# High and low halves of the weights side by side in one tile, features 1024 bytes apart

## The chip, the core and the metric

The kernel runs on one core of a Trainium2 chip. The time is the device time of one execution in microseconds (us). The kernel before was timed in three runs: median 1880.48 us, from 1879.29 to 1882.33 us.

## What is computed

The kernel computes one inference step of a decoder with two layers, for a prompt of 512 tokens and eight samples of eight tokens each, 576 token rows in all. The model is 1024 wide. Layer 0 mixes tokens by retention with four heads, layer 1 by multi-scale pooling. After the mixer each layer has cross-attention into 256 memory tokens and a gated feed-forward block with a causal convolution of width 3 between its two projections. Everything is float32. Cut to what the change touches, the reference is a row of products of token rows with weight matrices:

```python
proj = h @ w_in                      # retention: 1024 x 6144
out  = (silu(g) * o) @ w_out         # 2048 x 1024
k, v = hm @ wk, hm @ wv              # memory keys and values, 1024 x 1024 each
q    = h @ wq;  y = o @ wo           # cross-attention, 1024 x 1024 each
u    = h @ w_up                      # feed-forward up, 1024 x 5632
y    = (a * silu(gate)) @ w_down     # 2816 x 1024
```

## The kernel before

TensorE gets each float32 product as three products of rounded numbers. `split` (lines 227 to 233) rounds a float32 tile to its high half on ScalarE (the copy on line 229) and takes the rest as the low half on VectorE (the subtraction on line 230). `mm3` then issues high by high, high by low and low by high, all into one PSUM tile; each is one MATMUL on line 213 with one weight load of its own (LDWEIGHTS).

Weights come through `load_w` (line 254): a DMA on the SP queue brings 1024 float32 words for each of the 128 partitions into a tile `wraw`, and `split` makes the tiles `wh` and `wl` of it. `w_cols` asks for up to eight blocks of 128 input rows by 128 output columns; such a block is called a feature block here, and `kt` counts them. `w_rows` asks for wider pieces: four blocks of 256 columns, or two of 512. `run_tasks` works through a list of tasks and loads the weights of the next task before it issues the matmuls of this one, so that a load and a split lie beside the matmuls of the task before. `Weave` puts side work (attention, retention states, convolution rows) between the main matmuls by a clock of its own; it does not look at addresses.

In most projections the weights are the stationary operand and 576 token rows stream past them. A PSUM bank holds 512 of them, so `mm_kt` goes in two halves of 320 and 256 columns. One feature block is therefore six matmuls in a row, which the texts below call a six: weight tile high, high, low against 320 columns, then high, high, low against the other 256. A six streams 3 x 320 + 3 x 256 = 1728 columns. In the final down projection, in the first `w_xo` tasks of each head pair and in one task of the retention's output the two halves come apart, and a feature block is two threes. For the memory keys and values, the retention's values and the pooling mixer, the weight tile is the one that streams, and token rows are stationary.

Counted from the loops, the retention has 256 sixes in its q, k and gate projections and 120 in its output projection, the two cross-attentions have 192 and the two feed-forward blocks 1008.

Where a tile lies in the 128 partitions of SBUF is set by `new` (line 184): a tile is rounded up to a multiple of 32 words (128 bytes), and the names in `ODD`, `wh` and `wl` among them, start 16 words (64 bytes) in. So `wh` and `wl` take 1024 + 16 words, rounded up to 1056, which is 4224 bytes or 16.5 x 256. Pools lay out their buffers tag by tag. The pool `wA` (the retention's projections and 4 tasks of its output, 288 sixes) has two buffers of each tag, so a `wl` lies 2 x 4224 = 33 x 256 bytes behind its `wh`. The pool `wB` (all that follows, 1288 sixes) has three, so there it is 3 x 4224 = 49.5 x 256 bytes. Feature blocks of a `w_cols` tile are 512 bytes apart. The token rows that stream past lie 2560 bytes (10 x 256) apart in `xhl` and `yhl` (`ROW` is 640 words) and 2304 bytes (9 x 256) in `qo`; their second half starts 1280 bytes (5 x 256) further on, and all of them start at a multiple of 256 bytes.

In the built program this gives the following places of the stationary weights, as bytes past a multiple of 256. The sixes are counted by their pool.

| pool and buffers | `wh` | `wl` | sixes |
|---|---|---|---|
| `wB`, buffers 1 and 3 | 64 | 192 | 859 |
| `wB`, buffer 2 | 192 | 64 | 429 |
| `wA`, buffer 1 | 192 | 192 | 144 |
| `wA`, buffer 2 | 64 | 64 | 144 |

Of the kernel before, what the change touches and what calls it, by code (L numbers as in the profile page):

```python
# [11 lines left out]
F32R = mybir.dt.float32r  # L12
# [144 lines left out]
def body(ctx, tc, a, cdec):  # L157
# [4 lines left out]
    def f(t):  # L162
        return t.bitcast(F32)

    def open_pool(stack, name, bufs=1, **kw):
        return stack.enter_context(tc.tile_pool(name=name, bufs=bufs, reuse_waits="tile", **kw))
# [10 lines left out]
    def nm(s):  # L177
        cnt[0] += 1
        return f"{s}_{cnt[0]}"

    def acc():
        return P.acc.tile([128, 1024], F32, tag="acc", name=nm("acc"))
# [4 lines left out]
    def new(p, shape, tag, dt=F32, whole=True, **kw):  # L187


        n = 1  # L190
        for s in shape[1:]:
            n *= s
        o = LINE // 2 if tag in ODD else 0
        if n % LINE == 0 and o == 0 or not whole:
            return p.tile(shape, dt, tag=tag, name=nm(tag), **kw)
        t = p.tile([shape[0], -(-(n + o) // LINE) * LINE], dt, tag=tag, name=nm(tag), **kw)[:, o:o + n]
        if len(shape) == 2:
            return t
        ax = "abcd"[:len(shape) - 1]
        return t.rearrange(f"p ({' '.join(ax)}) -> p {' '.join(ax)}", **dict(zip(ax[1:], shape[2:])))  # L200

    def token_rows(p, shape, tag):

        return new(p, shape + [ROW], tag, F32R)[:, :, :, ROW - NT:]
# [22 lines left out]
    def split(hi, lo, src, scale=None, lo_pool=False):  # L227
        if scale is None:
            act.copy(hi, src)  # L229
            (pool if lo_pool else dve).tensor_tensor(out=lo, in0=src, in1=f(hi), op=ALU.subtract)  # L230
        else:
            act.activation(hi, src, AF.Copy, scale=scale)
            dve.scalar_tensor_tensor(out=lo, in0=src, scalar=scale, in1=f(hi), op0=ALU.mult, op1=ALU.subtract)
# [17 lines left out]
    class W:  # L251
        pool = first = None

    def load_w(src, shape):

        raw = new(W.pool, shape, "wraw", bufs=W.raw_bufs)
        dma.dma_start(out=raw, in_=src)
        wh = new(W.pool, shape, "wh", F32R, bufs=W.hl_bufs)
        wl = new(W.pool, shape, "wl", F32R, bufs=W.hl_bufs)
        split(wh, wl, raw)  # L260
        return wh, wl

    def w_cols(w, r0, nk, c0):
        return load_w(w[r0:r0 + nk * 128, c0:c0 + 128].rearrange("(k p) c -> p k c", p=128), [128, nk, 128])

    def w_rows(w, r0, nk, c0, n):
        return load_w(w[r0:r0 + nk * 128, c0:c0 + n].rearrange("(k p) c -> p k c", p=128), [128, nk, n])
# [3 lines left out]
    def mm_kt(ps, w, kt, xh, xl, first, last, halves=(0, 1)):  # L271

        wh, wl = w
        for s in halves:
            o, c, n = HALF[s]
            mm3(ps[:, o:o + n], wh[:, kt], wl[:, kt], xh[:, c:c + n], xl[:, c:c + n], first, last)
# [136 lines left out]
    def add_x(norm=None):  # L413
        def evac(i, ps):
            x = xt["x"]
            dve.tensor_tensor(out=x[:, i], in0=x[:, i], in1=flat(ps), op=ALU.add)  # L416
            if norm is not None:
                norm.feed(i)
        return evac
# [64 lines left out]
    wA = open_pool(sR, "wA", side="right")  # L484
    sM = ExitStack()
    W.pool = open_pool(sM, "wM")
    W.raw_bufs, W.hl_bufs = 4, 3
    mp = open_pool(sM, "mp")
    pool.memset(ones, 1.0)
# [58 lines left out]
    wv.spawn(prologue(), 2.0)  # L548

    def first_A():  # L550
        W.pool, W.raw_bufs, W.hl_bufs = wA, 2, 2
        return w_cols(a["w_ret_in"][0], 0, KT, 0)

    wv.run(run_tasks(mtasks0, first_A))
    wv.drain()
    sM.close()
# [227 lines left out]
    def y_load(ft, hi, lo):  # L784
        yr = new(ap1, [128, NT], "yr", bufs=2)
        dma.dma_start(out=yr, in_=y_dram[:, ft])
        split(hi, lo, yr)
        yk[ft] = hi, lo
# [100 lines left out]
    def out_tasks():  # L889
        tasks = []  # L890
        evac = add_x(first_norm)
        for grp in range(4):
            hold = {}
            for part, k0 in enumerate((8, 0, 4, 12)):
                def run(wt, part=part, k0=k0, grp=grp, hold=hold):
                    if part == 0:
                        if grp == 0:
                            wv.join(hd[3]["y2"])
                        hold.update({0: acc(), 1: acc()})
                    if grp == 0 and part == 1:  # L900
                        ya = token_rows(gp, [128, 2, KT], "xhl")
                        for ft in range(8):
                            y_load(ft, ya[:, 0, ft], ya[:, 1, ft])
                    if grp == 0 and part == 3:
                        wv.join(hd[3]["out"], hd[3]["bl"])
                        for i in range(4):
                            yk[12 + i] = y3[i // 2][:, 0, i % 2], y3[i // 2][:, 1, i % 2]
                        sA.close()
                        xt["pool"] = xp = open_pool(sX, "xp")
                        xt["x"] = new(xp, [128, KT, NT], "x")  # L910
                        for kt in range(KT):
                            dma.dma_start(out=xt["x"][:, kt], in_=x_dram[:, kt])
                        W.pool = open_pool(sX, "wB")
                        W.raw_bufs, W.hl_bufs = 3, 3
                    wh, wl = wt
                    if grp == 3 and part == 3:
                        first_norm.gcol = G_XA
                        for kt in range(4):
                            first_norm.split(kt)
                    both = (0, 1)  # L920
                    steps = [(m, kt, both) for kt in range(4) for m in range(2)]
                    if part == 3:
                        steps = [(m, kt, both) for m in range(2) for kt in range(4)]
                        if grp == 0:

                            steps = [(m, kt, (hv,)) for hv in both for m in range(2) for kt in range(4)]
                    for m, kt, halves in steps:
                        cc = slice(128 * m, 128 * m + 128)
                        mm_kt(hold[m], (wh[:, :, cc], wl[:, :, cc]), kt, *yk[k0 + kt], part + kt == 0,
                              part == 3 and kt == 3, halves)  # L930
                        yield
                        if part == 3 and kt == 3 and halves[-1]:
                            evac(2 * grp + m, hold[m])
                            if grp == 3 and m == 0:
                                first_norm.split(4)
                                first_norm.split(5)

                tasks.append(Task(lambda k0=k0, grp=grp: w_rows(w_out, 128 * k0, 4, 256 * grp, 256), run))
        return tasks

# [360 lines left out]
    def pool_mix(p, mtasks, norm, nnext):  # L1301
# [108 lines left out]
        def z_load():  # L1410
            return [load_w(a["pool_w"][0, 2 * g:2 * g + 2].rearrange("g (k p) c -> p (g k) c", p=128), [128, 4, 256])
                    for g in range(2)]
# [151 lines left out]
```

## Time and profile before

| what | value |
|---|---|
| median of the three runs | 1880.48 us |
| the profiled execution's own time | 1879.21 us |
| its span, first to last instruction | 1877.4 us |
| TensorE busy with matmuls | 1853.2 us, 13493 matmuls |
| VectorE busy | 1058.4 us |
| ScalarE busy | 735.0 us |

The profile is of one execution. Its span runs from the first instruction to the last; 1.8 us of the execution's time lie outside it. The ends of matmuls are modelled, so the length of a matmul's row is not what it costs: neighbours overlap. What a stretch of matmuls costs is read from starts, from one matmul's to another's. The timeline merges equal neighbours, so that the two first matmuls of a six stand as one row with x2, and the start of that row is the start of the six.

### The profile page before, as it was taken

What the parts mean: (1) busy time and instruction counts of PE and PEld (TensorE: products, weight loads), DVE (VectorE), ACT (ScalarE), POOL (GpSimd) and SP (SyncE); (2) the same over time, 40 slices, a digit from 0 to 9 for tenths busy, and PEclk for the clock granted to TensorE, in tenths of its full rate; (3) what the DMA queues carried; (4) which work ended last, traced back from release to release, by engine and by line L of the source; (5) the groups of instructions that cost most, each with busy time, mean ns of one, the idle gap of its engine ahead of it and who ended that gap; (6) DMA issues with size and microseconds to landing.
All of it is one profiled execution on the core that took longest, in us unless ns stands there. A gap on an engine that the chain in (4) does not pass through costs nothing.

```text
span 1877.4 us, 32680 instructions
## 1 busy us (share of the span) xinstructions
PE 1853.2 (99%) x13493; PEld 1740.2 (93%) x13493; DVE 1058.4 (56%) x1639; ACT 735.0 (39%) x1080; POOL 199.2 (11%) x384
## 2 busy tenths in 40 slices
PE   7999999999999999999999999999999999999998
PEld 6988888898899988999999999989898999999998
DVE  4645546464644545676367367674555664574567
ACT  5442332424423433543144134554443442342345
POOL 0211202011000100111011010001000110110110
PEclk9999999999999999999999999999999999999999
DMA  8635363555643555332332322546644232323224
GB/s 279 221 123 191 94 218 111 168 166 173 214 144 105 178 181 167 90 91 78 91 90 81 89 79 77 184 134 222 201 148 123 79 91 79 90 79 91 79 74 144
DMA packets 309691, 249.52 MB, mean 133 GB/s; under 512 B 12136, under 2 KB 267992, under 8 KB 309543
## 3 DMA queue, kind: packets, MB, share of 16 engines
q1 hardware_dynamic: 309543, 247.44, 42.5%
q8 instruction: 106, 1.74, 0.4%
q14 instruction: 42, 0.34, 0.1%
HBM read 210.51 MB, written 36.88 MB: 132 GB/s over the span
## 4 chain that ended last, share of the span: by engine, by line
PE 92%; issue 3%; DMA 2%; DVE 1%; ACT 1%; SPq 0%; POOL 0%; POOLq 0%; ACTq 0%; DVEq 0%
PE acc L213 77%; PE tp L213 11%; PE tp L219 3%; DMA wraw<-in_w_xk 1%; DMA wraw<-in_w_xq 0%; DMA cs<-in_c_rope 0%; DVE wl L230 0%; DMA y_dram<-yt 0%; DMA kvr<-in_cache_mem_v 0%; ACT wh L229 0%; DMA yr<-y_dram 0%; ACT m4k L472 0%; ACT z L229 0%; SPq L474 0%; POOL gn L342 0%
## 5 line engine op out<-in xcount | busy, mean ns | idle before, releaser
L213 PE MATMUL acc<-xhl,wh 128*128 128x320 f32 (+1 forms) x4608 | 919.9, 295 | 3.7 <-DVE x L416 1.9
L213 PEld LDWEIGHTS acc<-xhl,wh 128*128 128x128 f32 x4608 | 738.0, 188 | 15.3 <-issue 6.1
L213 PE MATMUL acc<-xhl,wl 128*128 128x320 f32 (+1 forms) x2304 | 675.2, 293 | 0.0
L229 ACT CAST wh<-wraw 128x1024 fp32r<-128x1024 f32 (+1 forms) x274 | 281.3, 1030 | 645.9 <-PE acc L213 501.6
L213 PEld LDWEIGHTS acc<-xhl,wl 128*128 128x128 f32 x2304 | 433.9, 188 | 0.0
L230 DVE TENSOR_TENSOR wl<-wraw,wh 128x1024 fp32r<-128x1024 f32 (+1 forms) x274 | 332.5, 1217 | 136.2 <-ACT wh L229 130.2
L213 PE MATMUL acc<-yhl,wh 128*128 128x320 f32 (+1 forms) x1408 | 278.5, 295 | 0.1
L213 PEld LDWEIGHTS acc<-yhl,wh 128*128 128x128 f32 x1408 | 223.7, 188 | 0.5 <-ACT yhl L229 0.4
L213 PE MATMUL acc<-yhl,wl 128*128 128x320 f32 (+1 forms) x704 | 205.9, 293 | 0.0
L1237 DVE SCALAR_TENSOR_TENSOR c<-e,cw,c 128x592 f32<-128x592 f32 x176 | 146.0, 832 | 3.8 <-ACT c L1235 0.3
L213 PEld LDWEIGHTS acc<-yhl,wl 128*128 128x128 f32 x704 | 132.6, 188 | 0.0
L416 DVE TENSOR_TENSOR x<-x,acc 128x576 f32<-128x576 f32 x64 | 48.2, 754 | 148.1 <-PE acc L213 147.9
L213 PE MATMUL acc<-qo,wh 128*128 128x320 f32 (+1 forms) x512 | 105.9, 302 | 0.6 <-ACT qo L229 0.6
L213 PE MATMUL acc<-wh,xhl 128*128 128x512 f32 (+1 forms) x320 | 96.7, 375 | 0.7 <-DVE r L600 0.7
L213 PE MATMUL acc<-wh,mT 128*128 128x512 f32 x256 | 86.7, 407 | 3.6 <-ACT wh L229 3.6
L213 PEld LDWEIGHTS acc<-qo,wh 128*128 128x128 f32 x512 | 81.0, 188 | 6.5 <-issue 4.1
L1235 ACT ACTIVATE c<-e,cw 128x592 f32<-128x592 f32 x88 | 77.6, 884 | 20.8 <-DVE e L1230 20.3
L1228 DVE TENSOR_TENSOR e<-acc,rstd_bc 128x64 f32<-128x64 f32 x88 | 19.5, 222 | 116.0 <-PE acc L213 115.8
L213 PE MATMUL acc<-qo,wl 128*128 128x256 f32 (+1 forms) x256 | 75.5, 296 | 0.0
L754 DVE SCALAR_TENSOR_TENSOR S<-S,tp 128x512 f32<-128x512 f32 x64 | 43.6, 682 | 51.0 <-PE tp L213 45.2
L213 PEld LDWEIGHTS acc<-wh,xhl 128*128 128x128 f32 x320 | 58.0, 188 | 11.4 <-issue 1.1
L1276 ACT ACTIVATE c<-c 128x592 f32<-128x592 f32 x44 | 30.8, 700 | 86.3 <-DVE c L1237 86.3
(280 smaller groups left out, 2224.9 us busy)
## 6 DMA issues: line engine op xcount, KB each, us to landing
wraw<-in_w_up SPq DMA_DIRECT2D x88, 512.0 KB, 3.7
wraw<-in_w_ret_in SPq DMA_DIRECT2D x48, 512.0 KB, 4.4
S<-in_state_ret SPq DMA_DIRECT2D x64, 256.0 KB, 3.8
o_ret_s<-S SPq DMA_DIRECT2D x64, 256.0 KB, 3.5
kvr<-in_cache_mem_k SPq DMA_DIRECT2D x64, 256.0 KB, 4.5
kvr<-in_cache_mem_v SPq DMA_DIRECT2D x64, 256.0 KB, 3.4
wraw<-in_w_down SPq DMA_DIRECT2D x32, 512.0 KB, 3.8
wraw<-in_w_down SPq DMA_DIRECT2D x24, 384.0 KB, 3.3
```

Source lines behind the costliest of these rows:

```text
L213: i = nc.tensor.matmul(out, lhsT, rhs, start=start, stop=stop)
L219: nc.tensor.transpose(out, in_, idn)
L229: act.copy(hi, src)
L230: (pool if lo_pool else dve).tensor_tensor(out=lo, in0=src, in1=f(hi), op=ALU.subtract)
L416: dve.tensor_tensor(out=x[:, i], in0=x[:, i], in1=flat(ps), op=ALU.add)
L754: dve.scalar_tensor_tensor(out=Su, in0=Su, scalar=cdec[h], in1=psu, op0=ALU.mult, op1=ALU.add)
L1228: dve.tensor_tensor(out=ev[:, 0:8, 2:10], in0=ps[:, A0:A0 + NS].rearrange("p (b t) -> p b t", t=T), in1=rstd_bc[:, 0:NS].rearrange("p (b t ...
L1235: act.activation(c, e[:, 2:2 + n], AF.Identity, scale=cw[:, 2, j:j + 1], bias=cw[:, 3, j:j + 1])
L1237: dve.scalar_tensor_tensor(out=c, in0=e[:, i:i + n], scalar=cw[:, i, j:j + 1], in1=c, op0=ALU.mult, op1=ALU.add)
L1276: act.activation(c, c, AF.Silu)
```

## The change

`load_w` asks for one tile `whl` in place of two. It has an axis of length 2 behind the feature axis: for each feature block the high words and then the low words. The two halves that it returns are views of it. For `w_cols` the feature blocks are then 1024 bytes apart and the low half lies 512 bytes behind the high one; for `w_rows` the distances are 2048 and 1024 bytes (256 columns) or 4096 and 2048 bytes (512 columns). `whl` is not among the names that start 64 bytes in; instead each weight pool gets one small tile ahead of its `whl` buffers and one behind them: none in the first pool, 16 and 16 words in `wA`, 144 and 48 words in `wB`. These hold no data.

```diff
     class W:
         pool = first = None
 
+        shift = rest = 0
+
     def load_w(src, shape):
 
         raw = new(W.pool, shape, "wraw", bufs=W.raw_bufs)
         dma.dma_start(out=raw, in_=src)
-        wh = new(W.pool, shape, "wh", F32R, bufs=W.hl_bufs)
-        wl = new(W.pool, shape, "wl", F32R, bufs=W.hl_bufs)
-        split(wh, wl, raw)
-        return wh, wl
+        if W.shift:
+            new(W.pool, [128, W.shift], "shift", whole=False)
+        t = new(W.pool, [shape[0], shape[1], 2, shape[2]], "whl", F32R, bufs=W.hl_bufs)
+        if W.shift:
+            new(W.pool, [128, W.rest], "rest", whole=False)
+            W.shift = 0
+        split(t[:, :, 0], t[:, :, 1], raw)
+        return t[:, :, 0], t[:, :, 1]
...
+    W.shift, W.rest = 0, 0
     W.raw_bufs, W.hl_bufs = 4, 3
...
-        W.pool, W.raw_bufs, W.hl_bufs = wA, 2, 2
+        W.pool, W.raw_bufs, W.hl_bufs, W.shift, W.rest = wA, 2, 2, 16, 16
...
                         W.pool = open_pool(sX, "wB")
+                        W.shift, W.rest = 144, 48
                         W.raw_bufs, W.hl_bufs = 3, 3
```

In the built program all five `whl` buffers of `wA` and `wB` start 832 bytes past a multiple of 1024. Past a multiple of 256 that is 64 for the high half of every feature block, and 64 for the low half too. The two small tiles keep `wB` as large as it was (25344 bytes); `wA` is 384 bytes smaller, and the tiles that the retention lays out beside it (`cs`, `xs`, `r`, `rt`, `qhl`, `khl`, `kdA`, `vhl`) move by that much.

The number of instructions of each kind stays. The order stays too, but for some fifty places on TensorE where a side matmul stands a few main matmuls earlier or later, and two neighbouring DMAs on SP that trade places. TensorE still waits for ScalarE before the high half and for VectorE before the low half, each for itself. At the first weight tile of the program (`wh_103` and `wl_104` before, `whl_103` now; `mT` holds the stationary memory rows) TensorE had:

```order
L213 MATMUL acc_138<-wh_103,mT_112 128x512 [waits Activation_49]
L213 MATMUL acc_138<-wl_104,mT_112 128x512 [waits DVE_49]
L213 MATMUL acc_138<-wh_103,mT_112 128x512 x2
L213 MATMUL acc_138<-wl_104,mT_112 128x512
L213 MATMUL acc_138<-wh_103,mT_112 128x512
```

Now TensorE has, at the same place:

```order
L213 MATMUL acc_136<-whl_103,mT_111 128x512 [waits Activation_49]
L213 MATMUL acc_136<-whl_103,mT_111 128x512 [waits DVE_49]
L213 MATMUL acc_136<-whl_103,mT_111 128x512 x4
L213 MATMUL acc_136<-whl_103,mT_111 128x512 [waits Activation_49]
L213 MATMUL acc_136<-whl_103,mT_111 128x512
```

Only the names moved; the first matmul still starts on ScalarE's word and the second on VectorE's.

## Rows read from the trace of the kernel before

**Rows 1.** The page, part 1: busy time, share of the span, instructions.
```profile
PE 1853.2 (99%) x13493; PEld 1740.2 (93%) x13493; DVE 1058.4 (56%) x1639; ACT 735.0 (39%) x1080; POOL 199.2 (11%) x384
```

**Rows 2.** The page, part 2: TensorE's granted clock, tenths, in 40 slices.
```profile
PEclk9999999999999999999999999999999999999999
```

**Rows 3.** The page, part 4: chain that ended last, by engine and by line.
```profile
PE 92%; issue 3%; DMA 2%; DVE 1%; ACT 1%; SPq 0%; POOL 0%; POOLq 0%; ACTq 0%; DVEq 0%
PE acc L213 77%; PE tp L213 11%; PE tp L219 3%; DMA wraw<-in_w_xk 1%; DMA wraw<-in_w_xq 0%; DMA cs<-in_c_rope 0%; DVE wl L230 0%; DMA y_dram<-yt 0%; DMA kvr<-in_cache_mem_v 0%; ACT wh L229 0%; DMA yr<-y_dram 0%; ACT m4k L472 0%; ACT z L229 0%; SPq L474 0%; POOL gn L342 0%
```

**Rows 4.** The page, part 5: groups by line; busy, mean ns, idle before, releaser.
```profile
L213 PE MATMUL acc<-xhl,wh 128*128 128x320 f32 (+1 forms) x4608 | 919.9, 295 | 3.7 <-DVE x L416 1.9
...
L229 ACT CAST wh<-wraw 128x1024 fp32r<-128x1024 f32 (+1 forms) x274 | 281.3, 1030 | 645.9 <-PE acc L213 501.6
...
L230 DVE TENSOR_TENSOR wl<-wraw,wh 128x1024 fp32r<-128x1024 f32 (+1 forms) x274 | 332.5, 1217 | 136.2 <-ACT wh L229 130.2
```

**Rows 5.** Busy us by engine in one up-projection task: PE, PEld, DVE, ACT, POOL.
```profile
853.29:859.56 6.27, 6.27 (x50) 6.27 (x49) 4.46 (x7) 3.22 (x4) 0.61 (x3) 1.00 0.30 86
```

**Rows 6.** Timeline, PE, up projection: start us, length, instruction; wB, buffers 1, 3, 2.
```profile
853.29 0.45 PE L213 MATMUL acc<-xhl,wh 128*128 128x320 f32 x2
854.09 0.45 PE L213 MATMUL acc<-xhl,wh 128*128 128x320 f32 x2
854.86 0.45 PE L213 MATMUL acc<-xhl,wh 128*128 128x320 f32 x2
...
859.56 0.45 PE L213 MATMUL acc<-xhl,wh 128*128 128x320 f32 x2
...
865.83 0.45 PE L213 MATMUL acc<-xhl,wh 128*128 128x320 f32 x2
...
871.29 0.45 PE L213 MATMUL acc<-xhl,wh 128*128 128x320 f32 x2
```

**Rows 7.** Timeline, PE, down projection, wB buffer 2.
```profile
886.19 0.45 PE L213 MATMUL acc<-yhl,wh 128*128 128x320 f32 x2
...
888.55 0.45 PE L213 MATMUL acc<-yhl,wh 128*128 128x320 f32 x2
```

**Rows 8.** Timeline, PE, retention, wA buffer 2, an early task.
```profile
87.04 0.46 PE L213 MATMUL acc<-xhl,wh 128*128 128x320 f32 x2
...
92.55 0.45 PE L213 MATMUL acc<-xhl,wh 128*128 128x320 f32 x2
```

**Rows 9.** Timeline, PE, retention, wA buffer 2, the end of a later task.
```profile
197.40 0.46 PE L213 MATMUL acc<-xhl,wh 128*128 128x320 f32 x2
...
201.37 0.40 PE L213 MATMUL acc<-wh,xhl 128*128 128x512 f32 x1
```

**Rows 10.** Timeline, PE, retention, wA buffer 1.
```profile
120.80 0.46 PE L213 MATMUL acc<-xhl,wh 128*128 128x320 f32 x2
...
124.77 0.46 PE L213 MATMUL acc<-xhl,wh 128*128 128x320 f32 x2
```

**Rows 11.** Timeline, PE, cross-attention output, first head pair.
```profile
735.88 0.45 PE L213 MATMUL acc<-qo,wh 128*128 128x320 f32 x2
...
736.67 0.45 PE L213 MATMUL acc<-qo,wh 128*128 128x320 f32 x2
```

**Rows 12.** Timeline, PE, cross-attention output, second head pair.
```profile
759.02 0.45 PE L213 MATMUL acc<-qo,wh 128*128 128x320 f32 x2
...
759.79 0.45 PE L213 MATMUL acc<-qo,wh 128*128 128x320 f32 x2
```

## The prediction

> **What bounds the kernel now.** I read the page first. TensorE is busy for 1853.2 of the span's 1877.4 us [rows 1], and the chain that ended last is TensorE for 92% of the span, 77% of it matmuls of line 213 into `acc` [rows 3]. The granted clock stands at nine tenths or more in all forty slices [rows 2], so all of this ran at the 2.4 GHz level and no stretch of 1.2 GHz is there to win back or to lose. In the groups by line the split of the weights is no limit: ScalarE's copy of a tile takes 1030 ns and VectorE's subtraction 1217 ns, and ScalarE stood idle for 645.9 us ahead of its copies, 501.6 us of that waiting for TensorE to give a buffer back [rows 4]. The weights are ready early, and TensorE waits for nothing large. A change of where weights lie can then act in one way only: on the time that a matmul takes when nothing is awaited.
>
> So I went to the timeline and measured sixes from start to start. At 2.4 GHz the 1728 columns of a six need 720 ns. No six is that short, and what it takes differs by the buffer that its weights lie in, though instructions and shapes are the same:
>
> - `wB` buffers 1 and 3 (high at 64, low at 192 past a multiple of 256): 16 sixes from 853.29 to 865.83, so 783.8 ns each [rows 6]. They alternate: the first takes 0.80 us, the next 0.77.
> - `wB` buffer 2 (192 and 64): 7 sixes from 865.83 to 871.29, 780.0 ns [rows 6]; in one stretch of the down projection 3 from 886.19 to 888.55, 786.7 ns [rows 7].
> - `wA` buffer 2 (64 and 64): 7 sixes from 87.04 to 92.55, 787.1 ns [rows 8]; in a later task 5 from 197.40 to 201.37, 794.0 ns [rows 9].
> - `wA` buffer 1 (192 and 192): 5 from 120.80 to 124.77, 794.0 ns [rows 10].
>
> These are undisturbed stretches: sixes that follow each other with no side work between.
>
> **Which part of the address counts.** This choice decides the forecast. Feature blocks of a task step by 512 bytes in the weights and by 2560 in the rows, which are 0 past a multiple of 256, and the 780.0 ns of buffer 2 do not move with them [rows 6]. The alternation in buffers 1 and 3 looks like an effect of the 512 bytes, since it goes with the parity of the feature block. It is not: in the cross-attention's output two sixes read the same weight place (address 108096 in the built program) and rows that both start at a multiple of 1024, and the one takes 0.79 us [rows 11], the other 0.77 [rows 12]. The alternation is a state that a six hands to the next. I therefore take the place past a multiple of 256, of the high and of the low half against the rows, as what counts, and the larger steps as without effect. That two reads of SBUF (rows for this matmul, weights for the next) get in each other's way is my reading of it; the times are the rows'.
>
> The Trainium skill says otherwise. Its page "TensorE: Matmul & The Clock Gate", section "Step-by-step: what each phase is for", gives TensorE two independent read ports into SBUF, so that loading the next weights takes nothing from the running matmul. By that rule no place matters, and the sum would be zero. This case's trace does not agree: the same six takes 780.0 or 794.0 ns by its buffer [rows 6, 10].
>
> **The change part by part.** After it, every six has high and low at 64 past a multiple of 256, in both pools, with the rows at 0. That is the pattern of `wA` buffer 2, which stood at 787.1 in one task and 794.0 in another [rows 8, 9]. Each of the two lasted for whole undisturbed stretches, and nothing in the profile says which one the long up projections will fall into; I take the middle, 790.6 ns, and keep both as ends.
>
> - `wB`, buffers 1 and 3: 859 sixes x (790.6 - 783.8) = +5.8 us (2.8 to 8.8).
> - `wB`, buffer 2: 429 x (790.6 - 780.0) = +4.5 us (3.0 to 6.0). The stretches at 786.7 make this a little too much [rows 7]; were half of them so, it would be 1.4 us less.
> - `wA`: 144 sixes at 794.0 and 144 between 787.1 and 794.0 become 790.6: -0.5 us (-1.5 to +0.5). In 64 sixes of the output projection the streamed rows move by half of 256 too (`xs`, `cs`, `r`, `rt`, `qhl`, `khl`), and then stand to the weights as in `wA` buffer 1: 64 x 3.4 = 0.2 us, left out.
> - Threes, where the halves come apart: 64 feature blocks of the `w_xo` tasks with two halves each (128 threes), 96 in the final down projection and 16 in the retention's output, 240 in all. At half of the six's change, some +4 ns each, +1.0 us (0.6 to 1.4).
> - Weight tiles that stream (memory keys and values, retention values, pooling): some 900 matmuls. Their high and low parts now start at one place too. Undisturbed 128x256 and 128x320 matmuls differ by a few ns from buffer to buffer, as above; at 1 ns each way that is 0 +- 0.9 us, and I take 0.
> - The split writes and reads rows of 128 words with gaps instead of 1024 in a row. The trace shows no such form of these two instructions; from 1030 and 1217 ns [rows 4] I bound it by nothing and by a tenth more, 0.22 us per tile. In an up-projection task of 6.27 us VectorE is busy 4.46 and ScalarE 3.22 [rows 5], so a tenth is hidden there by the matmuls of the task before. Were that cover gone, 274 tiles x 0.22 us = 60 us would show; it is not, since ScalarE waits 501.6 us for TensorE. Taken at 0.
> - Waits: as before, high and low half are awaited apart, and the last reader of a buffer is the same matmul. Nothing new is queued behind one. The traded pair of DMAs on SP and the moved side matmuls change no amount of work; 0.
>
> Sum: 5.8 + 4.5 - 0.5 + 1.0 = +10.8 us. Against the profiled execution's own time of 1879.2 us (span 1877.4 and 1.8 around it) that is 1890.0; that execution lies 1.3 us under the median of the three runs, so against 1880.5 it is 1891.3. I forecast **1891 us**. Its own range runs from all sixes at 787.1 (2.8 + 3.0 - 1.5 + 0.6 = +4.9, less the 1.4: +3.5) to all at 794.0 (8.8 + 6.0 + 0.5 + 1.4 = +16.7): 1884 to 1897.
>
> **The rivals.** *The short six everywhere (faster).* In buffers 1 and 3 each second six takes 0.77 us [rows 6], and in the up projection that is always the one whose high half starts 832 or 64 past a multiple of 1024. After the change all high halves start at 832. If that place, and not a state, makes a six short, all sixes take 773 ns: 859 x -10.8 = -9.3, 429 x -7 = -3.0, `wA` 288 x some -18 = -5.2, threes -1.3, so -18.8 us and 1861.7 us. It decides from the first up-projection task on. For it speaks the regular pattern of rows 6; against it rows 11 and 12, with equal places and unequal times, and that the low half no longer lies at 192.
>
> *The place doesn't matter, or the gains and losses cancel (no change).* If what sets the buffers apart is not their place, or if places 256 bytes apart are not alike and today's mean comes back, the time stays at 1880.5. For it: the differences are under 2% of a six. Against it: they keep to the buffer, as the equal pairs in rows 6 show to the hundredth of a us. (This is also what the page on TensorE named above would give, with its two ports.)
>
> *The distance of 512 bytes is a pattern of its own.* No six of before has its low half 512 bytes behind (the distances past a multiple of 1024 are 384 in `wB` and 256 in `wA`). If 512 counts differently from 256, a six could also take the 800 ns seen as the sum of a 0.80 us six without its short neighbour [rows 6]: 859 x 16 + 429 x 20 = 22 us, 1903. Nothing shows such a run of long sixes.
>
> **How the numbers follow.** The forecast's mechanism has 0.70, split evenly over its range; the short six 0.12; no change 0.13; the long six 0.05. Runs of this kernel spread by 0.1% to either side, so I count 0.2% (3.8 us, up to 1884.2) as the least that can be told from no change. Slower: 0.70 less 0.03 for its lower end, plus 0.05, is 0.72. Same: 0.13 + 0.03 less a little for cancelling with a remainder, 0.16. Faster: 0.12. The range leaves out the short six and the long one, and takes in no change: 1880 to 1898.
>
> **What would show it.** In the profile after, sixes of an up-projection task should start 0.79 us apart with no alternation, eight in 6.30 to 6.35 us for every buffer alike, where now a task takes 6.27 (buffers 1 and 3) or 6.24; TensorE's busy time should grow by about what the span grows by, the clock row should stay as it is, and ScalarE should still idle some 500 us behind TensorE. Wrong would be: sixes of 0.77 us in a row (the first rival); tasks of 6.25 us with a changed span (then the time went elsewhere, and the waits would name it); or a copy or subtraction much over 1030 and 1217 ns with TensorE waiting for it.

## The result and the profile after

The changed kernel takes 1893.4 us (median of 4 runs, 1891.2 to 1898.8) against 1881.4 for the kernel before on the same chip: a ratio of 1.0072, with a 95% interval of 1.0056 to 1.0089. (The two medians alone stand at 1.0064.) It is slower by 0.7%, and the 1891 of the forecast lies 2.4 us under it. The profiled execution took 1891.24 us with a span of 1889.4, that of before 1879.21 with 1877.4: +12.0 us.

The page of the kernel after, in the order of [rows 1 to 4]: busy times, granted clock, the chain that ended last by engine, and the three groups of the weights' path.

```profile
PE 1864.6 (99%) x13493; PEld 1751.0 (93%) x13493; DVE 1059.3 (56%) x1639; ACT 729.9 (39%) x1080; POOL 197.2 (10%) x384
...
PEclk9999999999999999999999999999999999999999
...
PE 89%; DMA 4%; issue 3%; DVE 2%; ACT 1%; POOL 0%; SPq 0%; POOLq 0%; ACTq 0%; DVEq 0%
...
L213 PE MATMUL acc<-xhl,whl 128*128 128x320 f32 (+1 forms) x6912 | 947.7, 295 | 1.4 <-ACT m4k L478 1.1
...
L229 ACT CAST whl<-wraw 128x1024 fp32r<-128x1024 f32 (+1 forms) x274 | 281.2, 1030 | 668.1 <-PE acc L213 535.8
L230 DVE TENSOR_TENSOR whl<-wraw,whl 128x1024 fp32r<-128x1024 f32 (+1 forms) x274 | 332.2, 1215 | 145.8 <-ACT whl L229 144.8
```

TensorE executes the same 13493 matmuls and is busy 11.4 us longer (1853.2 in [rows 1]), which is nearly all of the 12.0. The clock stays at the 2.4 GHz level in every slice, as in [rows 2]. The copy still takes 1030 ns and the subtraction 1215 (1217 in [rows 4]), and ScalarE still idles behind TensorE, 535.8 us of it. (The group of L213 can't be compared by its total: both halves have one name now, so it holds 6912 matmuls instead of 4608.) With the same number of matmuls, more of TensorE's time went into each.

Where both halves have one name the timeline merges the sixes of a task into one row, so I count instead. The next rows are two stretches of the feed-forwards in which TensorE does little but sixes, first of before, then of after. Columns: stretch, busy us of TensorE with its matmuls in brackets, granted clock, share of DMA, GB/s.

```profile
800.00:1120.00 320.00, 320.00 (x2456) 1.00 0.29 85
1470.00:1820.00 350.00, 350.00 (x2685) 1.00 0.29 84
```

```profile
800.00:1120.00 320.00, 320.00 (x2423) 1.00 0.29 85
1470.00:1820.00 350.00, 350.00 (x2649) 1.00 0.29 84
```

Length times 6 over the count is a six: 781.8 and 782.1 ns before, 792.4 and 792.8 after. (Matmuls cut at the ends are counted, so this lies up to 1 ns under the time from start to start, which is 793.4 in both stretches after. Eight sixes, an up-projection task, then take 6.35 us whatever their buffer, the upper end of what the prediction named as its sign.) The same two windows are read for every kernel below.

### The profile page after: what moved, and what is told of

Same layout as the page of the kernel before. It is cut to its first block, busy times and chain, and to the rows that moved or that the text cites. A ratio compares the mean times of both kernels' runs of the same rounds, so it can differ in the third digit from the quotient of the medians.

```text
span 1889.4 us, 32658 instructions
## 1 busy us (share of the span) xinstructions
PE 1864.6 (99%) x13493; PEld 1751.0 (93%) x13493; DVE 1059.3 (56%) x1639; ACT 729.9 (39%) x1080; POOL 197.2 (10%) x384
## 4 chain that ended last, share of the span: by engine, by line
PE 89%; DMA 4%; issue 3%; DVE 2%; ACT 1%; POOL 0%; SPq 0%; POOLq 0%; ACTq 0%; DVEq 0%
PE acc L213 75%; PE tp L213 11%; PE tp L219 3%; DMA wraw<-in_w_xk 1%; DMA bandf<-in_c_band 1%; DMA o_ret_s<-S 1%; DVE whl L230 1%; DMA y<-in_p_conv 1%; DMA yr<-y_dram 0%; ACT whl L229 0%; DMA wraw<-in_w_xq 0%; DMA wraw<-in_w_xv 0%; DMA y_dram<-yt 0%; DMA kvr<-in_cache_mem_v 0%; ACT xhl L232 0%
## 5 line engine op out<-in xcount | busy, mean ns | idle before, releaser
L213 PE MATMUL acc<-xhl,whl 128*128 128x320 f32 (+1 forms) x6912 | 947.7, 295 | 1.4 <-ACT m4k L478 1.1
L213 PEld LDWEIGHTS acc<-xhl,whl 128*128 128x128 f32 x6912 | 929.5, 188 | 12.7 <-issue 5.5
L229 ACT CAST whl<-wraw 128x1024 fp32r<-128x1024 f32 (+1 forms) x274 | 281.2, 1030 | 668.1 <-PE acc L213 535.8
L230 DVE TENSOR_TENSOR whl<-wraw,whl 128x1024 fp32r<-128x1024 f32 (+1 forms) x274 | 332.2, 1215 | 145.8 <-ACT whl L229 144.8
L213 PE MATMUL acc<-yhl,whl 128*128 128x320 f32 (+1 forms) x2112 | 284.4, 295 | 0.1
L213 PEld LDWEIGHTS acc<-yhl,whl 128*128 128x128 f32 x2112 | 279.9, 188 | 0.4 <-ACT yhl L229 0.4
L213 PE MATMUL acc<-qo,whl 128*128 128x256 f32 (+1 forms) x768 | 113.8, 300 | 0.6 <-ACT qo L229 0.6
L213 PEld LDWEIGHTS acc<-qo,whl 128*128 128x128 f32 x768 | 103.8, 188 | 7.9 <-issue 5.8
L213 PE MATMUL acc<-whl,xhl 128*128 128x512 f32 (+1 forms) x480 | 105.0, 373 | 0.8 <-DVE r L607 0.8
L213 PE MATMUL acc<-whl,mT 128*128 128x512 f32 x384 | 96.6, 404 | 5.6 <-ACT whl L229 3.8
L213 PEld LDWEIGHTS acc<-whl,xhl 128*128 128x128 f32 x480 | 82.0, 188 | 16.4 <-issue 1.2
L213 PEld LDWEIGHTS acc<-whl,mT 128*128 128x128 f32 x384 | 71.7, 192 | 22.8 <-ACT whl L229 4.6
L213 PE MATMUL tp<-vhl,kdA 128*128 128x512 f32 x216 | 53.5, 396 | 0.9 <-ACT on L648 0.9
```

The costliest lines, as they stand in the source:

```text
L213: i = nc.tensor.matmul(out, lhsT, rhs, start=start, stop=stop)
```

## Experiments

Theory: the time of a six hangs on the places of its high and low half past a multiple of 256 bytes against the rows, and at one pair of places it can keep one of several values. Rivals: the new distance in the tile (features 1024 bytes apart, the halves neighbours); the place past 1024; something around the sixes.

**1. All places, TensorE alone (`place`).** A bench ahead of the kernel's work; its core, for 16 pairs of tiles:

```diff
+for way in range(2):
+    ps = tp()
+    if way == 0:
+        one_mm(ps, hw[1][:, 0], bx[:, 0, 0, 0:512], True, True)
+    else:
+        for i in range(4):
+            one_mm(ps[:, 128 * i:128 * i + 128], one, one, True, True)
+    ps = acc()
+    for r in range(2):
+        for kt in range(KT):
+            ...  # one six: (h, xh), (h, xl), (l, xh) on 320, then on 256 columns
```

> The kernel after, with a bench of TensorE alone put ahead of its work, so only the bench is read and not the total. In it the six of a feature block (high, high, low weights on 320 columns, then on 256, rows at a multiple of 256 bytes) is repeated 16 times for each of the 16 pairs of places (high, low) from 0, 64, 128, 192 bytes past a multiple of 256, twice each: once behind one matmul of 512 columns, once behind four plain fp32 matmuls. Then high and low beside each other in one tile (features 1024 bytes apart, both at 64), then (64, 64) with the rows moved by 128 bytes, then the order high, low, high. Theory of places: (64, 192) 784 ns as a mean of 773 and 794 in turn; (192, 64) 780 or 787; (64, 64) 787 or 794; (192, 192) 794; beside each other the same as (64, 64) apart; rows moved by 128 bytes 794, as (192, 192). Rival, distance in the tile: (64, 64) apart 784 as (64, 192), and beside each other 787 to 794. Rival, places don't matter and something of the kernel around it set the six: all pairs within 3 ns of each other.

Timeline of TensorE, (64, 64) apart: `hb` is the high tile, and such a row begins a six. The second and the sixteenth six behind one matmul of 512 columns, then the second and the sixteenth behind four plain fp32 matmuls (eight rows of them in the trace):

```profile
149.16 0.45 PE L515 MATMUL acc<-bx,hb 128*128 128x320 f32 x2
...
160.17 0.45 PE L515 MATMUL acc<-bx,hb 128*128 128x320 f32 x2
160.96 1.05 PE L515 MATMUL tp<-one 128*128 128x128 f32 x8
...
162.65 0.45 PE L515 MATMUL acc<-bx,hb 128*128 128x320 f32 x2
...
173.76 0.46 PE L515 MATMUL acc<-bx,hb 128*128 128x320 f32 x2
```

14 sixes in 11.01 us are 786.4 ns; 14 in 11.11 are 793.6. One pair of places, the same instructions and addresses, and two values, each kept to the end. High and low beside each other in one tile (`hl`, 96 matmuls, again behind the one and the other):

```profile
439.29 12.75 PE L515 MATMUL acc<-bx,hl 128*128 128x320 f32 x96
451.88 1.05 PE L515 MATMUL tp<-one 128*128 128x128 f32 x8
452.68 12.94 PE L515 MATMUL acc<-bx,hl 128*128 128x320 f32 x96
465.46 0.40 PE L515 MATMUL tp<-bx,hb 128*128 128x512 f32 x1
```

From 439.29 to 451.88 are 16 sixes of 786.9; from 452.68 to 465.46, less 0.88 for the first behind fp32, 15 of 793. The neighbourhood and the 1024 bytes add nothing. (64, 192) alternates as in [rows 6]:

```profile
215.63 0.45 PE L515 MATMUL acc<-bx,hb 128*128 128x320 f32 x2
216.43 0.45 PE L515 MATMUL acc<-bx,hb 128*128 128x320 f32 x2
217.20 0.45 PE L515 MATMUL acc<-bx,hb 128*128 128x320 f32 x2
...
223.47 0.45 PE L515 MATMUL acc<-bx,hb 128*128 128x320 f32 x2
```

10 sixes in 7.84 us, 784. From the same view: (192, 64) 787 both times; (192, 192) 793.4; (64, 64) with the rows moved by 128 bytes 793, both times, which is as expected but no proof, since (64, 64) takes 793 without the move too. Of the pairs that this kernel doesn't use, (0, 0) and (128, 64) took 800; none of the 16 had a mean under that of (64, 192). The order high, low, high was not faster: 800 at (64, 192), 793 at (192, 64) and (64, 64). Nearly nothing runs beside the bench; in this row the busy times are those of TensorE, its weight loads, VectorE, ScalarE and GpSimd, then clock, DMA share and GB/s:

```profile
30.00:570.00 540.00, 540.00 (x4101) 539.12 (x4100) 0.00 (x0) 8.49 (x40) 0.00 (x0) 1.00 0.00 1
```

The rivals of distance and of surroundings fall: they wanted 784 for (64, 64) apart, or one value for all.

**2. Another place past 1024 (`moved_512`).** The kernel after, high halves of the pool `wB` at 320 instead of 832.

```diff
-                        W.shift, W.rest = 144, 48
+                        W.shift, W.rest = 16, 176
```

> The kernel after, with the weight tiles of the feed-forward and cross-attention moved by 512 bytes, so that their high halves lie 320 instead of 832 bytes past a multiple of 1024, and still 64 past a multiple of 256. Theory of places past 256: as the kernel after, 1.005 to 1.009 of before, the six at 787 or 794. Rival, the place past 1024 counts: another six; 773 would give about 0.99 of before, and any mean below 785 would speak for it.

```profile
800.00:1120.00 320.00, 320.00 (x2422) 1.00 0.29 85
```

1.0063 (1.0047 to 1.0078) of before, and a six of 792.7: no difference from the kernel after. A step of 512 bytes doesn't count, as the prediction took it.

**3. The places without the neighbourhood (`apart_64_64`, `apart_192_64`, `apart_64_192`).** The kernel before with both halves one behind the other in a tile of 2112 words, features 512 bytes apart as before, all tiles at one pair of places. The edit for (64, 64); the others differ in the offsets (in `wA`, which begins 128 past a multiple of 256, they are chosen for the same places):

```diff
-        wh = new(W.pool, shape, "wh", F32R, bufs=W.hl_bufs)
-        wl = new(W.pool, shape, "wl", F32R, bufs=W.hl_bufs)
+        n = shape[1] * shape[2]
+        t = W.pool.tile([128, 2112], F32R, tag="whl", name=nm("whl"), bufs=W.hl_bufs)
+        wh, wl = (t[:, o:o + n].rearrange("p (k c) -> p k c", k=shape[1]) for o in ((16, 1040) if W.hl_bufs == 3 else (48, 1072)))
```

> The kernel before, with high and low weights in halves of 4096 bytes one behind the other in one tile (features 512 bytes apart as before), all of them at (64, 64). Theory of places: as slow as the kernel after without anything lying beside each other, 1.004 to 1.009 of before, the six at 787 or 794. Rival, the distance of 1024 bytes or the neighbourhood of high and low costs the time: 0.999 to 1.001, the six at a mean of 784.

> The same with all high halves at 192 and all low halves at 64 bytes past a multiple of 256. Theory of places: the six at 780 or 787, against a mean of 784.6 over the kernel before: 1565 sixes by -4.6 to +2.4 ns, -7 to +4 us, 0.996 to 1.002 of before, and 6 to 20 us under the one with (64, 64). Rival, distance: the same time as (64, 64) apart.

> All weights at (64, 192), high and low halves one behind the other in a tile, nothing added. Theory: 784 ns in every stretch, a mean of 773 and 794, against 784.6 over the kernel before: -1 us, 0.9985 to 1.0005 of before. Rival, the new tiles cost time of their own: above 1.0015.

The first window of each, in this order:

```profile
800.00:1120.00 320.00, 320.00 (x2423) 1.00 0.29 84
```

```profile
800.00:1120.00 320.00, 320.00 (x2443) 1.00 0.29 85
```

```profile
800.00:1120.00 320.00, 320.00 (x2453) 1.00 0.29 85
```

(64, 64): a six of 792.4 and 1.0054 (1.0039 to 1.0069), the slowdown with nothing beside each other. (64, 192): 782.7 and 1.0004 (0.9994 to 1.0015), so the new tile costs nothing by itself. (192, 64): 785.9 and 1.0031 (1.0019 to 1.0043), over the range expected, and only 3 us under (64, 64) by the medians where 6 to 20 were expected; the totals alone hardly tell these two apart, the sixes do. In its trace the feed-forwards stand at 786.7 from start to start, and over 100 sixes, nearly all outside them, at 806.7, a third lasting value that the bench had not shown. In the trace of (64, 192) long and short sixes no longer go with the place past 1024: among undisturbed sixes with the high half at 832, 240 are long and 209 short. So that place does not make the alternation; that a six hands it to the next, as [rows 11, 12] were read, fits.

**4. What chooses the value (`states`).** The bench again: sixes behind a fixed start (four fp32 matmuls or four transposes) and one or two extra matmuls, for two pairs of places; then the 16 pairs with the low rows at other places than the high ones.

```diff
+for q, cols_ in nudge:
+    one_mm(tp()[:, 0:cols_], hw[q][:, 0], bx[:, 0, 0, 64:64 + cols_], True, True)
```

> The kernel after with another bench of TensorE ahead of its work; only the bench is read. First part: 9 sixes at (64, 64) and then at (192, 64), behind four plain fp32 matmuls or four transposes, with nothing between or with one or two matmuls of 64 to 512 columns at 64 or 192 bytes. Theory of lasting states: at one pair of places the six settles on one of a few values and keeps it until something else comes between; what stands directly ahead chooses it. So (64, 64) at 794 behind four fp32 matmuls alone and at 787 with one of 512 columns between, as in the first bench, and (192, 64) on 780, 787 or 807, each kept over the 9 sixes. Rival, the value is set by the place alone and what wandered in the kernels came from what ran beside it (DMA, the other engines): (64, 64) the same within 2 ns in all 24 groups, and (192, 64) too. Second part: the 16 pairs again with the low rows at 64, 128 or 192 bytes while the high rows stay at 0. Theory of places relative to each other: other pairs of values than with both rows at 0, between 773 and 800, and none under 765, since 576 x 3 columns took 765 in the sums of the row durations (three 320s of 141.7 and three 256s of 113). Rival, the rows' place doesn't matter: the same values as with both at 0.

At (64, 64) twelve of the 24 groups settled at 786.6 to 786.8 and twelve at 793.2 to 793.4; at (192, 64) seventeen at 786.7 and seven at 780.0. One of these seven, with one matmul of 320 columns at 64 bytes between, its second and its ninth six:

```profile
244.20 0.39 PE L514 MATMUL tp<-bx,hb 128*128 128x320 f32 x1
...
245.22 0.45 PE L514 MATMUL acc<-bx,hd 128*128 128x320 f32 x2
...
250.68 0.45 PE L514 MATMUL acc<-bx,hd 128*128 128x320 f32 x2
```

7 sixes in 5.46 us, 780.0. A value is chosen by what stands ahead and then kept, with next to nothing running beside TensorE. With the low rows moved, the pairs took other means, 786.6 to 806.6 and none lower: (64, 64), for one, stood at 800.0 with the low rows at 64, behind either start. So the place of the rows counts too, and nothing was to be gained there.

**5. One small matmul in the kernel after (`after_nudge_64`).** 64 columns that nobody reads, behind the fp32 matmuls that spread the norm's factors, into free columns of the first one's PSUM tile (`p0`); four times in the kernel.

```diff
+        if xhl is not None:
+            nc.tensor.matmul(p0[:, 128:192], xhl[:, 0, 0, 16:144], xhl[:, 0, 1, 0:64], start=True, stop=True)
```

> The kernel after, with one more matmul of 64 columns whose output nobody reads, four times in the kernel: directly behind the plain fp32 matmuls that spread the norm's factors, ahead of the cross-attentions' and the feed-forwards' long stretches of sixes. Theory of lasting states: the stretches of 433 and 467 sixes, which stood at 793.4 ns in the kernel after, stand at 786.7, as behind the same two things in the bench; 900 x -6.7 = -6.0 us, a ratio to before of about 1.0035 (1.002 to 1.005). Rival, the value of a stretch comes from its place or from what runs beside it: 793.4 as before, 1.006 to 1.008.

The spot in the second feed-forward, and the two windows:

```profile
1462.60 1.52 PE L213 MATMUL tp<-qt,ones 64*128 64x64 f32 x10
1463.87 0.28 PE L366 MATMUL tp<-xhl 128*128 128x64 f32 x1
1463.98 4.18 PE L213 MATMUL acc<-xhl,whl 128*128 128x320 f32 x30
```

```profile
800.00:1120.00 320.00, 320.00 (x2443) 1.00 0.30 86
1470.00:1820.00 350.00, 350.00 (x2672) 1.00 0.30 85
```

785.9 in both (786.7 from start to start) instead of 792.4 and 792.8, and 1.0039 (1.0027 to 1.0051) where 1.0035 was expected. By the ratios nearly half of the slowdown, 0.33 of 0.72%, was the value that the long stretches had fallen into; by the two profiled executions it is a third, 4.0 of 12.0 us.

**6. The same for (192, 64) (`apart_nudge_320`, `mixed_nudge`).** 320 columns at 192 bytes in the same four spots; in the second kernel (192, 64) holds in the feed-forwards alone and (64, 192) elsewhere. The first line below is in both kernels, the others tell the second from the first.

```diff
+            nc.tensor.matmul(p0[:, 128:448], xhl[:, 0, 0, 48:176], xhl[:, 0, 1, 0:320], start=True, stop=True)
...
-        wh, wl = (... for o in ((1072, 16) if W.hl_bufs == 3 else (16, 1072)))
+        wh, wl = (... for o in W.at)
```

> The kernel with high and low halves one behind the other in a tile at (192, 64), with one more matmul of 320 columns at 192 bytes in the same four spots. Theory of lasting states: the stretches of 510 and 467 sixes go from 786.7 to 780.0 ns, the lowest value of the benches; -6.5 us and 0.6 us for the four matmuls themselves, a ratio to before of about 1.000 (0.998 to 1.0015). Rival: 786.7 as without, 1.003.

> As the last one in the feed-forwards; everywhere else all weights at (64, 192), which had one value in the bench, a mean of 784, and not the 807 that (192, 64) fell into for some 100 sixes outside the feed-forwards. Theory: 974 sixes at 780 instead of the 784.6 of before (-4.5 us), the others at 784 (0 to -0.5), 0.6 us for the four matmuls: about 0.998 of before (0.9965 to 0.9995), faster than before and than the change. Rival: the feed-forwards at 786.7, 1.001 to 1.002.

Both missed: 1.0034 (1.0022 to 1.0047) and 1.0028 (1.0017 to 1.0038), and the feed-forwards stayed at 786.7. The first window of the second kernel; that of the first has the same count of matmuls:

```profile
800.00:1120.00 320.00, 320.00 (x2443) 1.00 0.29 84
```

The bench's fp32 matmuls had their weights and rows at 0, those of the kernel have them at 128; that is one difference, and if it were the cause, the choice would reach back past the extra matmul. No run tests it. In any case the bench's list doesn't carry over. (The profiled execution of the second kernel was its shortest of twelve, 1879.8 against a median of 1885.8; its trace doesn't show what the others spent.)

**7. A list made in the kernel itself (`nudges`).** The kernel of (192, 64), with 72 kinds of extra matmuls ahead of tasks of the feed-forwards.

```diff
+            if W.nudges and i >= 2:
+                ...
+                for q, n in W.nudges.pop(0):
+                    ...
+                    nc.tensor.matmul(tp()[:, 0:n], wt, xhl[:, 0, 1, 0:n], start=True, stop=True)
             yield from t.run(w)
```

> The kernel with high and low halves one behind the other at (192, 64), with one or two more matmuls ahead of most tasks of the feed-forwards, 72 kinds in turn: 32 to 512 columns, with the task's high weights, its low ones, both, or others at 0 or 128 bytes; only the sixes between them are read, not the total. It looks for what moves a running stretch from 786.7 to 780.0 ns, which 320 columns behind the fp32 matmuls did in the bench and did not in the kernel. Theory of lasting states: each kind leaves the next sixes at 780, 787 or 807, kept up to the next extra matmul; some kinds change the value and some don't. Rival, in the feed-forward something else holds the sixes at 786.7: that value behind all 72.

Two pieces of the timeline (each L213 row is eight sixes up to the next L305 row):

```profile
851.54 0.31 PE L305 MATMUL tp<-xhl,whl 128*128 128x320 f32 x1
851.69 6.61 PE L213 MATMUL acc<-xhl,whl 128*128 128x320 f32 x48
858.14 0.34 PE L305 MATMUL tp<-xhl,whl 128*128 128x384 f32 x1
...
922.29 0.27 PE L305 MATMUL tp<-xhl,whl 128*128 128x224 f32 x1
922.40 6.48 PE L213 MATMUL acc<-yhl,whl 128*128 128x320 f32 x48
928.71 0.28 PE L305 MATMUL tp<-xhl,whl 128*128 128x256 f32 x1
928.83 6.41 PE L213 MATMUL acc<-yhl,whl 128*128 128x320 f32 x48
935.08 0.30 PE L305 MATMUL tp<-xhl,whl 128*128 128x320 f32 x1
```

Behind 320 columns with high weights eight sixes take 6.45 us (806.7 each past the first), behind 224 columns with low weights 6.31 (786.7), behind 256 with low weights 6.25 (780.0). Every one of the 72 left the sixes at one of these three, kept until the next: 45 at 786.7, 18 at 780.0 and 9 at 806.7. The rival, 786.7 behind all, falls.

**8. The version that this points to (`mixed_780`).** (192, 64) in the feed-forwards, (64, 192) elsewhere, and 256 columns with the low weights once per feed-forward, ahead of its third task.

```diff
+            if W.rows is not None and i == 2:
+                nc.tensor.matmul(tp()[:, 0:256], w[1][:, 0], W.rows[:, 0, 1, 0:256], start=True, stop=True)
+                W.rows = None
             yield from t.run(w)
```

> The kernel with (192, 64) in the feed-forwards and (64, 192) elsewhere again, without the matmuls of 320 columns; in their place one matmul of 256 columns with the low weights, once per feed-forward, ahead of its third task, which in the run of 72 kinds took a stretch from 786.7 to 780.0. Theory of lasting states: some 420 and 450 sixes at 780.0 instead of 786.7, -5.8 us, and 0.4 us less for extra matmuls: a ratio to before of about 0.9995 (0.998 to 1.001), 0.002 to 0.004 under the version with 320 columns. Rival, the step from 786.7 to 780.0 hung on the matmuls ahead of it in that run: 786.7 again, 1.0015 to 1.003.

```profile
786.77 9.70 PE L213 MATMUL acc<-xhl,whl 128*128 128x320 f32 x72
796.31 0.28 PE L302 MATMUL tp<-xhl,whl 128*128 128x256 f32 x1
796.43 6.84 PE L213 MATMUL acc<-xhl,whl 128*128 128x320 f32 x51
```

```profile
800.00:1120.00 320.00, 320.00 (x2464) 1.00 0.30 86
1470.00:1820.00 350.00, 350.00 (x2694) 1.00 0.29 84
```

779.2 and 779.5 by the count, 780.2 and 780.1 from start to start, over 428 and 464 sixes; 1879.08 us, 0.9996 (0.9987 to 1.0005) of before. That is 0.003 under the version with 320 columns, and below the changed kernel by its full 0.7%. Against the kernel before it can't be told from no change: that one has (64, 192) in most sixes, a mean of 784, and the 4 ns gained in the feed-forwards are partly lost where the memory's transposes throw 38 sixes to 806.7.

## Why the prediction was right

**What bounds the kernel, and where the change can act.** Right. The split's form cost nothing, no new wait appeared, the clock did not move; TensorE's busy time took nearly all of the growth.

**Which part of the address counts.** Right, and now shown: a six takes the same values with the tile moved by 512 bytes (experiment 2) and with other distances between halves and features (1, 3), and other values at other places of the weights (1) or of the low rows (4). The Trainium skill's page "TensorE: Matmul & The Clock Gate", section "Step-by-step: what each phase is for", gives TensorE two independent read ports, so that a weight load takes nothing from the running matmul; by that rule no place should matter. The runs show 780 to 807 ns by place and by what stood ahead. That reads of rows and weights get in each other's way stays my reading; no run here separates the two reads.

**The sum.** Taken over the sixes that stand at the same place of the program in both traces, from start to start and undisturbed:

- `wB`, buffers 1 and 3: 783.7 to 792.9 ns, +9.2 where I had +6.8. Over 859 sixes this is +7.9 us instead of +5.8: the term that was mis-sized. I took the middle of the two values of (64, 64), and the long stretches fell into the upper one.
- `wB`, buffer 2: 781.5 to 792.7. I had 780.0 to 790.6; both ends were low, so the difference, +11.2 against +10.6, moves little: +4.8 us instead of +4.5.
- `wA`: 793.6 to 790.7 at (192, 192), 791.3 to 791.9 at (64, 64): -0.4 and +0.1 us over 144 sixes each, against -0.5 in all.
- With the threes and streaming weights left as they stood (+1.0 and 0) this sums to 13.4, over the +12.0 of the profiled executions; I had +10.8.

Starts show where the 12.0 us lie. The first matmul of each feed-forward and the first behind it (behind the second, the first of the final down projection), before and then after:

```profile
774.54 0.39 PE L213 MATMUL acc<-xhl,wh 128*128 128x320 f32 x1 [0.94 <-DVE x L416]
1194.34 0.40 PE L213 MATMUL acc<-wh,mT 128*128 128x512 f32 x1
1444.73 0.39 PE L213 MATMUL acc<-xhl,wh 128*128 128x320 f32 x1 [0.94 <-DVE x L416]
1824.04 0.30 PE L213 MATMUL acc<-yhl,wh 128*128 128x320 f32 x1
```

```profile
774.85 0.31 PE L213 MATMUL acc<-xhl,whl 128*128 128x320 f32 x1
1201.18 0.40 PE L213 MATMUL acc<-whl,mT 128*128 128x512 f32 x1
1451.59 0.30 PE L213 MATMUL acc<-xhl,whl 128*128 128x320 f32 x1
1836.03 0.31 PE L213 MATMUL acc<-yhl,whl 128*128 128x320 f32 x1
```

The first feed-forward took 419.80 us before and 426.33 after; the second, up to its final down projection, 379.31 and 384.44. That is 11.7 us in these two. The threes of the final down projection took 44.1 us in both traces, and the two stretches that hold the cross-attentions did not grow (170.4 and 169.8 us, then 250.4 in both). So what the sum has for the threes there and for the sixes of the cross-attentions is not seen in the total. That +10.8 came near +12.0 is in part luck: one term was too small and others too large.

The choice of the middle was the freest step. Experiment 5 puts its price on it: with the long stretches at 786.7 the same layout gives 1.0039 instead of 1.0072.

**The rivals.** The short six everywhere (1861.7) fell: 773 ns is half of a pair with 794, and the place past 1024 does not make it. No change fell with the interval. The long six of 800 ns exists, at (0, 0) and (128, 64), but not at the pair to which this change moves.

## What to carry to other kernels

Where TensorE hardly waits, compare the same instruction sequence from buffer to buffer: an unchanged count of matmuls with a longer busy time at the same granted clock points to where operands lie, and a change of layout should be planned by the places of weights and rows together. Repacking tiles changes those places silently, so keep them, or measure the alternatives with a bench in the same kernel. And give a forecast both values where the trace shows that a sequence can settle on two: which one it takes depended here on a few matmuls ahead of it.

## What the runs showed of the hardware that was not expected

- One unchanged sequence of six matmuls has several lasting values: 786.7 and 793.4 ns at (64, 64); 780.0, 786.7 and 806.7 at (192, 64). They lie 6.7 ns or a multiple of it apart, 16 cycles at 2.4 GHz.
- One matmul of 64 or 256 columns, about 0.1 us, moved more than 400 sixes behind it from one value to another, some 3 us per stretch.
- An extra matmul of 320 columns brought (192, 64) to 780.0 in the bench and not in the kernel. Why, and what inside the chip holds the value, stays open.
